# An encoder block on one core: the planner's engine durations reset, and a charge for each change of TensorE tile size

## The chip, the cores and the metric

The kernel runs on one core of a Trainium2 chip. The metric is the device time of one execution in microseconds (us). The times shown are the median and the span of several runs; the profile is of one further execution.

## What is computed

One layer of a hybrid encoder, 256 positions of 2048 features in float32. A normalised input `h` goes through one combined projection; the parts feed multi-head latent attention (8 heads), a bidirectional RWKV-7 recurrence (16 heads of 64) and gates. Both branches are projected, gated, added, projected once more, normalised and added to the input.

```python
h = rms_norm(x, g_pre)
proj = h @ w_in                       # 2048 x 10688
...
y_mla = mla_attention(q_nope, q_rope, k_nope, k_rope, v_mla)
...
def step(st, inp):                    # RWKV-7, forward and backward over time
    r_t, w_t, k_t, v_t, a_t, b_t = inp
    sa = jnp.einsum('dbhij,dbhj->dbhi', st, a_t)
    st = st * w_t[..., None, :] + sa[..., None] * b_t[..., None, :] + v_t[..., None] * k_t[..., None, :]
    y = jnp.einsum('dbhij,dbhj->dbhi', st, r_t)
    return st, y
...
u_mla = (y_mla * jax.nn.silu(z_mla)) @ w_br_mla
u_rwkv = (y_rwkv * jax.nn.silu(z_rwkv)) @ w_br_rwkv
merged = jax.nn.sigmoid(gate_mla) * u_mla + jax.nn.sigmoid(gate_rwkv) * u_rwkv
out = merged @ w_out
x = (x + rms_norm(out, g_post)).astype(x.dtype)
```

## The kernel before, in words

**Dense work.** Every projection is done with each operand split into a high and a low part, in three matmuls: high by high (L390), high by low of the input (L391), low of the weights by high (L392). Weights arrive on SP's queue in chunks of 128x1024 (three `raw` buffers). ScalarE casts a chunk to its high part `whi` (L321), VectorE subtracts to get the low part `wlo` (L324), and TensorE uses a chunk in 24 matmuls of 128x256 (`cm_task`, L390 to L392). In the text these matmuls of the shared projections are the dense matmuls. The projections after the attention norms have lines of their own: L1073 to L1082 for `wkv`, L1125 to L1127 for `wq`; the output projection has L1328 to L1330.

**The recurrence.** The 16 heads are worked in four quads, one after the other, each for both directions. For a quad, `front_k`, `front_d` and `front_v` prepare decays and keys on ScalarE and VectorE, with small matmuls for the low-rank projections (L678 to L680), head sums (L581, L582) and transposes (L642). Then `chunks_of` does, over four chunks of 64 positions:

- the Gram stage on TensorE: four times a group at L791 (64x128 tiles), masked on VectorE (L185, `g<-m,mask`), and four transposes at L799, copied by ScalarE (L778);
- the inverse of triangular 32x32 blocks on VectorE: transposes at L812 and L813, 60 small operations at L185 (`tmp`, `u`), transposes at L840, L842 and L844; then two groups of 32x32 matmuls on TensorE, L854 and L856, each copied at L861;
- the scan over the four chunks, a chain in which TensorE and the copies take turns: L886 (128x64 tiles), L906 and L908 (64x64), copies L910 and L912, L917 (64x64), copies L919 and L921, L935 and L938 (128x64), and the new state `z` (L185).

A quad's L938 must be done before the Gram stage of the next. The first `wkv` projection also waits for the last quad.

**What sets the order.** Every piece of work is a generator that yields (engine, duration, time when ready, kind) before it issues. The class `Streams` plans with these numbers: at each step it takes, for each engine, the waiting piece of best rank among those that could start within a small slot of the first, then the one that starts earliest over all engines, lets it issue, and moves that engine's free time on by the duration. A fourth field on ScalarE names the activation table, with 1.3 charged for a change. The planner runs when the program is built; each engine then works its instructions in the order in which they were issued, and waits only for data and buffers. So the durations in the source change nothing but the order. Those that the change touches are:

```python
steps.append((len(mt) * 3 * 0.109, mm) + ...)   # L394, dense step
e = yield ("P", 1.2)                            # L788, Gram group
yield ("D", cD(n * w) + 0.02)                   # L828, L830, inverse, 60 times a quad
yield ("D", 1.14)                               # L839, L841, L843, transposes
e = yield ("P", 0.9)                            # L848, 32x32 groups
e = yield ("P", 0.7, max(e0, e1))               # L913, in the scan
```

Of the kernel before, what the change touches and what calls it, by code (L numbers as in the profile page):

```python
# [16 lines left out]
D = 2048  # L17
# [26 lines left out]
class Streams:  # L44
# [32 lines left out]
    def run(self, until=None):  # L77
        while self.live and not (until and until()):
            moved = True
            while moved:  # L80
                moved = False
                for s in list(self.live):
                    while s in self.live and s[3][0] in "WT" and (s[3][0] == "T" or s[3][1]()):
                        if s[3][0] == "T":
                            s[2] = max(s[2], s[3][1])
                        self._next(s, s[2])
                        moved = True
            if until and until():
# [24 lines left out]
            self.used[e] += cost  # L113
            s[2] = start + cost + self.LAG[e]
            self._next(s, s[2])
# [33 lines left out]
def encoder_block_kernel(  # L149
# [215 lines left out]
    def cm_task(src, nk, xhi, xlo, mt, wd, end, kc=4, load_fn=None, ready=None, kready=None, k_first=0,  # L365
# [7 lines left out]
        for i, k0 in enumerate(k0s):  # L373
# [201 lines left out]
    def head_sums(v, m):  # L575
# [3 lines left out]
        yield ("P", 0.44)  # L579
# [46 lines left out]
    def front_v(Q):  # L626
# [9 lines left out]
        for q in range(0, 4, 2):  # L636
            m = yield from MB.take()
            mv = m.rearrange("p (a c) -> p a c", a=4)
            e = yield ("P", 0.45)
# [13 lines left out]
    def front_d(Q, d):  # L653
# [18 lines left out]
        for i, (t, src, bcol) in enumerate(((th, tw, V_W0F + 8 * d), (tha, ta, V_A0F + 8 * d))):  # L672
            m = yield from MB.take()
            yield ("P", 0.66)
# [86 lines left out]
    def chunks_of(Q):  # L761
# [20 lines left out]
        for d in range(2):  # L782
            for j in range(2):
# [4 lines left out]
                e = yield ("P", 1.2)  # L788
# [8 lines left out]
                e = yield ("P", 0.6)  # L797
# [13 lines left out]
        yield ("D", 2.3)  # L811
# [13 lines left out]
        for j in range(1, 31):  # L825
            n, w = 31 - j, (j + 1) // 2
            o = tmp[:, 0:n * w].rearrange("p (a b) -> p a b", b=w)
            yield ("D", cD(n * w) + 0.02)  # L828
            tt(o, bc(Ai[:, j + 1:32, j:j + 1], [128, n, w]), bc(Tc[:, j:j + 1, 0:w], [128, n, w]), ALU.mult)
            yield ("D", cD(n * w) + 0.02)  # L830
# [8 lines left out]
        yield ("D", 1.14)  # L839
        dve.transpose(out=tm[B1].rearrange("p u s -> p s u"), in_=Ai[B1].rearrange("p t s -> p s t"))  # L840
        yield ("D", 1.14)  # L841
        dve.transpose(out=Gu[B1, :, 0:32].rearrange("p u t -> p t u"), in_=Ai[B1])  # L842
        yield ("D", 1.14)  # L843
        dve.transpose(out=Gu[B2, :, 32:64].rearrange("p u t -> p t u"), in_=Ai[B2])  # L844
        for step in range(2):
# [3 lines left out]
            e = yield ("P", 0.9)  # L849
# [7 lines left out]
            for j in range(4):  # L857
                on, cost = (("A", cA(256)), ("D", cD(256)))[j % 2]
# [30 lines left out]
        for q in range(4):  # L889
# [3 lines left out]
            if q == 0:  # L893
                mu = yield from MB.take()
                pu = mu[:, 0:256].rearrange("p (a c) -> p a c", a=4)
                e = yield ("P", 0.7)
                by_v(pu, q)
            m = yield from MB.take()
            py = m[:, 0:256].rearrange("p (a c) -> p a c", a=4)
            if q:  # L900
                e = yield ("P", 0.75)
# [7 lines left out]
            e0 = yield ("A", cA(256), e)  # L909
            act.copy(rhs[Hs, 1], pu[R64[0]])  # L910
            e1 = yield ("D", cD(256), e)
            dve.tensor_copy(rhs[Hs, 0], pu[Hs])  # L912
            e = yield ("P", 0.7, max(e0, e1))  # L913
# [4 lines left out]
            e1 = yield ("A", cA(256), e)  # L918
            act.copy(uv[Hs, 0:4], pu[R64[0]])  # L919
            e2 = yield ("D", cD(256), e)  # L920
# [8 lines left out]
            e = yield ("P", 0.2 + cost + (0.5 if q < 3 else 0.0), eu)  # L929
# [107 lines left out]
    def wkv_task(g):  # L1037
# [23 lines left out]
        for k0 in range(0, 4, 2):  # L1061
# [4 lines left out]
            for k in range(k0, k0 + 2):  # L1066
# [17 lines left out]
                steps.append((12 * 0.109, mm))  # L1084
# [12 lines left out]
    def wq_task(g):  # L1097
# [8 lines left out]
        for k0 in range(0, 4, 2):  # L1106
# [11 lines left out]
            for k in range(k0, k0 + 2):  # L1118
# [10 lines left out]
                steps.append((9 * 0.109, mm))  # L1129
# [32 lines left out]
    def head(g, i):  # L1162
# [7 lines left out]
        for t in range(2):  # L1170
# [3 lines left out]
            yield ("P", 0.55)  # L1174
# [130 lines left out]
    def out_task(n, wo_v=w_out.rearrange("(k p) c -> p k c", p=128)):  # L1305
# [13 lines left out]
        for k0 in range(0, KT, 2):  # L1319
# [4 lines left out]
            for k in range(k0, k0 + 2):  # L1324
# [7 lines left out]
                for t in range(2):  # L1332
                    steps[t if n == 3 and k0 >= 6 else 0].append((3 * 0.216, lambda b, hi, lo, mm=mm, t=t: mm(b, hi, lo, t)))
# [314 lines left out]
```

## Time and profile before

| | us |
|---|---|
| median of 3 runs | 885.38 |
| lowest, highest | 884.04, 886.46 |
| the profiled execution | 883.63 |
| its span, first to last instruction | 881.9 |
| TensorE (PE) busy in the span | 851.0 |
| VectorE (DVE) busy | 660.1 |
| ScalarE (ACT) busy | 501.0 |
| mean granted TensorE clock | 0.984 of full speed |

Busy time counts a matmul from its start to its modelled end; matmuls overlap, so the step from one start to the next is what a matmul takes of the time. A row of waits has the waiting engine and line, what it waited for, the sum, the number and the longest. A row of windows has a stretch and for each engine its busy time in it, with the number of instructions; then the granted clock, the share of the DMA engines, and what they moved.

### The profile page before, as it was taken

The numbers are of one execution on the slowest core, as the hardware profiler recorded it, in microseconds if no ns is written. First come the engines' busy times: TensorE is split into PE (matmuls) and PEld (weight loads), VectorE is DVE, ScalarE is ACT, GpSimd is POOL, SyncE is SP. The second block draws the span as 40 slices with busy tenths as digits, with TensorE's granted clock in tenths as the row PEclk, the third lists the DMA queues.
The fourth block names the chain that finished last, engine by engine and source line by source line (L and its number), as shares of the span: only waits on it lengthen the run. The fifth ranks groups of instructions, "written<-read, shape, count | busy, mean of one in ns | idle before, by whom it ended". The sixth has DMA issues, their size and how long they took to land.

```text
span 881.9 us, 19393 instructions
## 1 busy us (share of the span) xinstructions
PE 851.0 (97%) x8112; PEld 814.6 (92%) x8112; DVE 660.1 (75%) x1082; ACT 501.0 (57%) x797; POOL 30.8 (3%) x66
## 2 busy tenths in 40 slices
PE   8999999999999999999999997979999999999996
PEld 8999999899999999999899896879999999998884
DVE  5878898867988867998868988566868556775554
ACT  6688554478444478554478543656857433444442
POOL 4110000000000000000001000000000000000000
PEclk9999999999999999999999999879999999999999
DMA  9566546534746534646525365125545675655563
GB/s 283 167 176 182 165 123 193 164 84 113 194 136 192 165 84 121 192 134 189 161 63 147 97 192 167 32 69 171 168 115 144 206 277 186 191 178 198 195 196 117
DMA packets 123528, 139.41 MB, mean 158 GB/s; under 512 B 6704, under 2 KB 110512, under 8 KB 123056
## 3 DMA queue, kind: packets, MB, share of 16 engines
q1 hardware_dynamic: 121664, 135.16, 51.9%
q0 software_dynamic: 768, 1.57, 0.6%
q8 instruction: 63, 1.03, 0.5%
q10 hardware_dynamic: 1008, 1.44, 0.5%
q14 instruction: 25, 0.20, 0.1%
HBM read 136.05 MB, written 2.10 MB: 157 GB/s over the span
## 4 chain that ended last, share of the span: by engine, by line
PE 88%; DVE 6%; ACT 3%; DMA 1%; issue 1%; POOL 0%; SPq 0%; DVEq 0%; ACTq 0%
PE d L390 19%; PE d L391 18%; PE d L392 18%; PE m L1329 2%; PE m L1330 2%; PE m L1328 2%; PE m L392 2%; PE m L391 2%; PE m L390 2%; PE m L791 2%; DVE wlo L324 2%; PE d L1329 1%; PE d L1330 1%; PE d L1328 1%; PE m L917 1%
## 5 line engine op out<-in xcount | busy, mean ns | idle before, releaser
L321 ACT CAST whi<-raw 128x1024 fp32r<-128x1024 f32 (+3 forms) x252 | 253.1, 1006 | 255.9 <-PE d L391 147.0
L324 DVE TENSOR_TENSOR wlo<-raw,whi 128x1024 fp32r<-128x1024 f32 (+3 forms) x250 | 292.3, 1170 | 121.2 <-ACT whi L321 119.3
L390 PE MATMUL d<-hhi,whi 128*128 128x256 f32 (+1 forms) x1264 | 366.4, 290 | 3.1 <-ACT u L1265 1.9
L392 PE MATMUL d<-hhi,wlo 128*128 128x256 f32 (+1 forms) x1264 | 358.5, 284 | 0.0
L391 PE MATMUL d<-hlo,whi 128*128 128x256 f32 (+1 forms) x1264 | 358.3, 283 | 0.1
L390 PEld LDWEIGHTS d<-hhi,whi 128*128 128x128 f32 (+1 forms) x1264 | 241.5, 191 | 7.6 <-ACT u L1265 2.1
L391 PEld LDWEIGHTS d<-hlo,whi 128*128 128x128 f32 (+1 forms) x1264 | 241.9, 191 | 0.4 <-DVE hlo L188 0.3
L392 PEld LDWEIGHTS d<-hhi,wlo 128*128 128x128 f32 (+1 forms) x1264 | 241.8, 191 | 0.3 <-DVE wlo L324 0.2
L185 DVE TENSOR_TENSOR work<-work,work 128x512 f32<-128x512 f32 (+5 forms) x64 | 38.9, 613 | 6.7 <-ACT work L429 4.5
L185 DVE TENSOR_TENSOR u<-u,tmp 128x30 f32<-128x30 f32 (+7 forms) x120 | 29.9, 250 | 3.1
L185 DVE TENSOR_TENSOR tmp<-u 128x30 f32<-128x30 f32 (+7 forms) x120 | 29.9, 249 | 3.0
L390 PE MATMUL d<-b,whi 128*128 128x256 f32 x96 | 27.1, 282 | 0.0
L392 PE MATMUL d<-b,wlo 128*128 128x256 f32 x96 | 27.1, 282 | 0.0
L392 PE MATMUL d<-ar,wlo 128*128 128x256 f32 x96 | 26.9, 281 | 0.0
L391 PE MATMUL d<-ar,whi 128*128 128x256 f32 x96 | 26.9, 280 | 0.0
L391 PE MATMUL d<-work,whi 128*128 128x256 f32 x96 | 26.9, 280 | 0.0
L390 PE MATMUL d<-ar,whi 128*128 128x256 f32 x96 | 26.9, 280 | 0.0
L1328 PE MATMUL m<-whi,hhi 128*128 128x512 f32 x60 | 23.3, 389 | 0.0
L1329 PE MATMUL m<-wlo,hhi 128*128 128x512 f32 x60 | 23.3, 389 | 0.0
L1330 PE MATMUL m<-whi,hlo 128*128 128x512 f32 x60 | 23.3, 389 | 0.0
L390 PE MATMUL m<-hhi,whi 128*128 128x256 f32 x80 | 23.2, 290 | 0.0
L392 PE MATMUL m<-hhi,wlo 128*128 128x256 f32 x80 | 22.6, 282 | 0.0
(335 smaller groups left out, 1536.9 us busy)
## 6 DMA issues: line engine op xcount, KB each, us to landing
raw<-in_w_in_dram SPq DMA_DIRECT2D x160, 512.0 KB, 3.9
raw<-in_w_out_dram SPq DMA_DIRECT2D x32, 512.0 KB, 3.6
raw<-in_w_br_mla_dram SPq DMA_DIRECT2D x16, 512.0 KB, 3.6
raw<-in_w_br_rwkv_dram SPq DMA_DIRECT2D x16, 512.0 KB, 3.4
raw<-in_mla_wkv_b_dram SPq DMA_DIRECT2D x8, 512.0 KB, 3.6
raw<-in_mla_wq_b_dram SPq DMA_DIRECT2D x8, 384.0 KB, 3.3
raw<-in_w_in_dram SPq DMA_DIRECT2D x7, 384.0 KB, 5.4
g<-in_x_dram SPq DMA_DIRECT2D x2, 1024.0 KB, 7.4
```

The costliest lines, as they stand in the source:

```text
L185: dve.tensor_tensor(out=o, in0=a, in1=b, op=op)
L321: act.copy(dst(c.hi), src(raw))
L324: eng.tensor_tensor(out=dst(c.lo), in0=src(raw), in1=dst(c.hi).bitcast(F32), op=ALU.subtract)
L390: pe.matmul(o, hi[:, c:c + m], xhi(k), start=k == k_first and i % 2 == 0, stop=False)
L391: pe.matmul(o, hi[:, c:c + m], xlo(k), start=False, stop=False)
L392: pe.matmul(o, lo[:, c:c + m], xhi(k), start=False, stop=last)
L791: pe.matmul(m[:, q * 128:q * 128 + 128], z.kb[R64[h], d, j, q], z.ar[d][R64[h], j, q], start=q == 0, stop=q == 3)
L917: pe.matmul(pu[R64[i], a], G[Hs, st, q, 0:64], rhs[Hs, st % 2, st // 2], start=a == 0, stop=a == 3)
L1328: pe.matmul(banks[t], hhi[:, k, T], hi, start=k == 0, stop=False)
L1329: pe.matmul(banks[t], hhi[:, k, T], lo, start=False, stop=False)
L1330: pe.matmul(banks[t], hlo[:, k, T], hi, start=False, stop=k == KT - 1)
```

## The change

The durations of about thirty yields are replaced. Dense matmuls go from 0.109 to 0.119 each, those of the output projection from 0.216 to 0.227. The VectorE transposes of the inverse go from 1.14 to 2.0 and its 60 small operations rise by 0.095 each; copies out of PSUM rise by 0.07 to 0.11; the small TensorE groups of the Gram stage, the inverse and the scan mostly fall. These groups now also name their tile size, and the planner charges 0.2 whenever TensorE goes from one tile size to another. No instruction's operands change. Lines after the class are 6 further down in the new kernel (L854 becomes L860).

```diff
@@ -53,6 +53,7 @@
         self.live = []
         self.used = dict.fromkeys("PADGS", 0.0)
         self.table = None
+        self.mode = "128x128"
...
@@ -106,7 +107,12 @@
             _, s, start = best
             e, cost = s[3][0], s[3][1]
-            if len(s[3]) > 3 and s[3][3] != self.table:
+            if e == "P":
+
+                mode = s[3][3] if len(s[3]) > 3 else "128x128"
+                cost += 0.2 * (mode != self.mode)
+                self.mode = mode
+            elif len(s[3]) > 3 and s[3][3] != self.table:
                 self.table = s[3][3]
                 cost += 1.3
             self.free[e] = start + cost
...
-                steps.append((len(mt) * 3 * 0.109, mm) + (((lambda k=k: kready(k)),) if kready else ()))
+                steps.append((len(mt) * 3 * 0.119, mm) + (((lambda k=k: kready(k)),) if kready else ()))
...
-                e = yield ("P", 1.2)
+                e = yield ("P", 0.9, None, "64x128")
...
-            yield ("D", cD(n * w) + 0.02)
+            yield ("D", cD(n * w) + 0.115)
...
-        yield ("D", 1.14)
+        yield ("D", 2.0)
...
-            e = yield ("P", 0.9)
+            e = yield ("P", 0.5, None, "32x32")
...
-            e = yield ("P", 0.7, max(e0, e1))
+            e = yield ("P", 0.48, max(e0, e1), "64x64")
...
```

**First place: TensorE at the inverse of quad 3.** `u` and `g` are the blocks of the inverse, `whi` and `wlo` the split weights, `hhi` and `hlo` the split input. Before:

```order
L390 MATMUL d_111<-hhi_75,whi_19_81 128x256
L391 MATMUL d_111<-hlo_76,whi_19_81 128x256
L392 MATMUL d_111<-hhi_75,wlo_22_84 128x256
L854 MATMUL m_108<-u_200_5915,g_198_5851 32x32 x32
L856 MATMUL m_109<-g_198_5851,u_200_5915 32x32 x32
L390 MATMUL d_112<-hhi_75,whi_20_82 128x256
```

Now:

```order
L398 MATMUL d_110<-hhi_75,wlo_22_84 128x256
L860 MATMUL m_107<-u_204_5657,g_198_5523 32x32 x32
L396 MATMUL d_110<-hhi_75,whi_20_82 128x256
L397 MATMUL d_110<-hlo_76,whi_20_82 128x256
L398 MATMUL d_110<-hhi_75,wlo_23_85 128x256
```

Before, the two groups of the inverse follow each other; now 24 dense matmuls stand between them, of which the first three are shown.

**Second place: TensorE at the end of the scan of quad 3.** `uv` and `work` hold the copies, `bdr` the matrix of the head sums. Before:

```order
L908 MATMUL m_107<-ar_5618,z_6780 64x64 x2
L917 MATMUL m_105<-work_131_3775,g_198_5851 64x64 x8
L938 MATMUL m_107<-g_198_5851,uv_5706 64x64 x8
L581 MATMUL m_109<-work_214_6869,bdr_68 128x256
L582 MATMUL m_109<-work_215_6870,bdr_68 128x256
```

Now:

```order
L398 MATMUL d_111<-hhi_75,wlo_22_84 128x256
L944 MATMUL m_109<-g_198_5523,uv_5483 64x64 x8
L396 MATMUL d_111<-hhi_75,whi_19_81 128x256
L397 MATMUL d_111<-hlo_76,whi_19_81 128x256
L398 MATMUL d_111<-hhi_75,wlo_22_84 128x256
```

Before, the last three steps of the chain and the head sum follow each other, and the first `wkv` matmul comes after four head-sum matmuls. Now 6 dense matmuls stand before L944 and 24 behind it, and 108 in all up to the first `wkv` matmul.

## Rows read from the trace of the kernel before

**Rows 1.** The page, busy us of each engine, its share of the span, its instructions.

```profile
PE 851.0 (97%) x8112; PEld 814.6 (92%) x8112; DVE 660.1 (75%) x1082; ACT 501.0 (57%) x797; POOL 30.8 (3%) x66
```

**Rows 2.** The page, tenths busy in 40 slices of the span, and granted clock.

```profile
DVE  5878898867988867998868988566868556775554
...
PEclk9999999999999999999999999879999999999999
```

**Rows 3.** Waits of TensorE, 480 to 600 us: total us, times, longest.

```profile
PE m L856 <- DVE g L844: 4.4, 1, 4.4
...
PE m L581 <- ACT work L429: 1.9, 1, 1.9
PE m L917 <- DVE work L912: 1.8, 1, 1.8
PE m L854 <- DVE u L840: 1.6, 1, 1.6
...
PE m L938 <- ACT uv L919: 0.8, 1, 0.8
PE m L791 <- DVE g L185: 0.7, 1, 0.7
```

**Rows 4.** Windows at quad 3: length, busy by engine (x), PEclk, DMA.

```profile
486.60:495.60 9.00, 7.10 (x83) 5.73 (x81) 9.00 (x16) 4.54 (x8) 0.00 (x0) 1.00 0.45 123
540.00:545.00 5.00, 3.36 (x86) 3.05 (x85) 4.60 (x6) 2.41 (x3) 0.00 (x0) 1.00 0.71 209
545.00:550.00 5.00, 0.49 (x5) 0.35 (x4) 4.67 (x4) 0.59 (x2) 0.00 (x0) 0.69 0.33 107
550.00:555.00 5.00, 2.84 (x68) 2.47 (x67) 1.27 (x3) 2.44 (x6) 0.00 (x0) 0.50 0.01 3
555.00:560.00 5.00, 5.00 (x55) 4.51 (x54) 0.43 (x1) 2.32 (x5) 0.00 (x0) 0.79 0.00 0
575.00:580.00 5.00, 3.27 (x88) 2.81 (x86) 3.72 (x8) 3.67 (x7) 0.61 (x2) 1.00 0.31 105
580.00:585.00 5.00, 2.23 (x33) 1.80 (x33) 4.05 (x6) 3.48 (x8) 0.00 (x0) 0.60 0.10 23
585.00:590.00 5.00, 4.86 (x23) 4.66 (x23) 3.11 (x6) 1.53 (x4) 0.00 (x0) 0.50 0.24 85
```

**Rows 5.** Windows by stage: busy PE, PEld, DVE, ACT, POOL; the sum of ten.

```profile
117.30:169.00 51.70, 51.70 (x490) 51.53 (x489) 47.35 (x92) 24.41 (x29) 0.12 (x1) 1.00 0.61 172
169.00:201.00 32.00, 30.58 (x540) 27.79 (x540) 22.00 (x38) 22.18 (x43) 2.58 (x5) 1.00 0.39 107
201.00:247.50 46.50, 46.50 (x420) 45.31 (x415) 40.27 (x57) 29.42 (x48) 1.78 (x5) 1.00 0.55 153
247.50:301.40 53.90, 53.90 (x506) 53.56 (x505) 46.16 (x86) 26.67 (x30) 0.00 (x0) 1.00 0.57 159
...
467.50:496.60 29.10, 27.20 (x251) 25.77 (x250) 25.67 (x36) 22.55 (x38) 1.10 (x3) 1.00 0.46 128
496.60:549.30 52.70, 46.77 (x446) 46.25 (x444) 47.64 (x92) 21.94 (x23) 0.00 (x0) 0.98 0.57 160
sum 431.90, PE 419.88 PEld 406.49 DVE 362.24 ACT 247.53 POOL 11.94; mean PE 41.99 PEld 40.65 DVE 36.22 ACT 24.75 POOL 1.19
```

**Rows 6.** Timeline of TensorE in quad 0's scan: start us, us, what.

```profile
176.54 0.68 PE L917 MATMUL m<-work,g 64*64 64x64 f32 x16 [0.38 <-DVE work L912]
177.15 0.38 PE L390 MATMUL d<-hhi,whi 128*128 128x256 f32 x1
...
178.33 0.28 PE L390 MATMUL d<-hhi,whi 128*128 128x256 f32 x1
178.45 0.28 PE L391 MATMUL d<-hlo,whi 128*128 128x256 f32 x1
...
178.78 0.69 PE L935 MATMUL m<-uv,b 128*64 128x64 f32 x16
```

**Rows 7.** The page, costliest groups: busy us, mean ns, idle before.

```profile
L324 DVE TENSOR_TENSOR wlo<-raw,whi 128x1024 fp32r<-128x1024 f32 (+3 forms) x250 | 292.3, 1170 | 121.2 <-ACT whi L321 119.3
```

More of the change, by code (lines that the diff above doesn't have):

```diff
@@ L578, in head_sums @@
         yield from two_parts(v, w2d(hi), w2d(lo))
-        yield ("P", 0.44)
+        yield ("P", 0.476)
         for j in range(2):
@@ L638, in front_v @@
             mv = m.rearrange("p (a c) -> p a c", a=4)
-            e = yield ("P", 0.45)
+            e = yield ("P", 0.75)
             for d, vs in ((0, v), (1, vr)):
@@ L673, in front_d @@
             m = yield from MB.take()
-            yield ("P", 0.66)
+            yield ("P", 0.715)
             for j in range(2):
@@ L796, in chunks_of @@
                 m = yield from MB.take()
-                e = yield ("P", 0.6)
+                e = yield ("P", 0.72)
                 for q in range(4):
@@ L810, in chunks_of @@
         Af = Ai.rearrange("p t s -> p (t s)")
-        yield ("D", 2.3)
+        yield ("D", 4.1)
         dve.transpose(out=Af[B1], in_=Gu[B1, :, 0:32].rearrange("p u t -> p t u"))
@@ L827, in chunks_of @@
             o = tmp[:, 0:n * w].rearrange("p (a b) -> p a b", b=w)
-            yield ("D", cD(n * w) + 0.02)
+            yield ("D", cD(n * w) + 0.115)
             tt(o, bc(Ai[:, j + 1:32, j:j + 1], [128, n, w]), bc(Tc[:, j:j + 1, 0:w], [128, n, w]), ALU.mult)
-            yield ("D", cD(n * w) + 0.02)
+            yield ("D", cD(n * w) + 0.115)
             tt(Tc[:, j + 1:32, 0:w], Tc[:, j + 1:32, 0:w], o, ALU.add)
@@ L838, in chunks_of @@
         dve.memset(Af[Hs, ::33], 1.0)
-        yield ("D", 1.14)
+        yield ("D", 2.0)
         dve.transpose(out=tm[B1].rearrange("p u s -> p s u"), in_=Ai[B1].rearrange("p t s -> p s t"))
-        yield ("D", 1.14)
+        yield ("D", 2.0)
         dve.transpose(out=Gu[B1, :, 0:32].rearrange("p u t -> p t u"), in_=Ai[B1])
-        yield ("D", 1.14)
+        yield ("D", 2.0)
         dve.transpose(out=Gu[B2, :, 32:64].rearrange("p u t -> p t u"), in_=Ai[B2])
@@ L857, in chunks_of @@
             for j in range(4):
-                on, cost = (("A", cA(256)), ("D", cD(256)))[j % 2]
+                on, cost = (("A", cA(256) + 0.07), ("D", cD(256) + 0.09))[j % 2]
                 yield (on, cost, e)
@@ L895, in chunks_of @@
                 pu = mu[:, 0:256].rearrange("p (a c) -> p a c", a=4)
-                e = yield ("P", 0.7)
+                e = yield ("P", 0.48, None, "128x64")
                 by_v(pu, q)
@@ L900, in chunks_of @@
             if q:
-                e = yield ("P", 0.75)
+                e = yield ("P", 0.5, None, "64x64")
                 for dj in range(4):
@@ L908, in chunks_of @@
                         pe.matmul(py[R64[h], dj], Z[R64[h], dj], ar[R64[h], 64:128], start=dj == 0, stop=False)
-            e0 = yield ("A", cA(256), e)
+            e0 = yield ("A", cA(256) + 0.08, e)
             act.copy(rhs[Hs, 1], pu[R64[0]])
-            e1 = yield ("D", cD(256), e)
+            e1 = yield ("D", cD(256) + 0.11, e)
             dve.tensor_copy(rhs[Hs, 0], pu[Hs])
-            e = yield ("P", 0.7, max(e0, e1))
+            e = yield ("P", 0.48, max(e0, e1), "64x64")
             for a in range(4):
@@ L917, in chunks_of @@
                     pe.matmul(pu[R64[i], a], G[Hs, st, q, 0:64], rhs[Hs, st % 2, st // 2], start=a == 0, stop=a == 3)
-            e1 = yield ("A", cA(256), e)
+            e1 = yield ("A", cA(256) + 0.08, e)
             act.copy(uv[Hs, 0:4], pu[R64[0]])
-            e2 = yield ("D", cD(256), e)
+            e2 = yield ("D", cD(256) + 0.11, e)
             dve.tensor_copy(uv[Hs, 4:8], pu[Hs])
@@ L928, in chunks_of @@
             cost = 1.0 if q < 3 else 0.5
-            e = yield ("P", 0.2 + cost + (0.5 if q < 3 else 0.0), eu)
+            e = yield ("P", cost + (0.5 if q < 3 else 0.0), eu, "128x64")
             if q < 3:
@@ L1082, in mm @@
                         pe.matmul(o, kvhl[:, 1, k, T], vh, start=False, stop=(k == 3 and t == 1))
-                steps.append((12 * 0.109, mm))
+                steps.append((12 * 0.119, mm))
             parts.append((load, plain(1024), steps))
@@ L1127, in mm @@
                         pe.matmul(o, wl, qhl[:, 0, k], start=False, stop=(k == 3 and i != 0))
-                steps.append((9 * 0.109, mm))
+                steps.append((9 * 0.118, mm))
             parts.append((load, pairs, steps))
@@ L1173, in head @@
             sc = p2(m)[:, 0]
-            yield ("P", 0.55)
+            yield ("P", 0.59)
             pe.matmul(sc, qh[:, T], kT[:, 0], start=True, stop=False)
@@ L1332, in out_task @@
                 for t in range(2):
-                    steps[t if n == 3 and k0 >= 6 else 0].append((3 * 0.216, lambda b, hi, lo, mm=mm, t=t: mm(b, hi, lo, t)))
+                    steps[t if n == 3 and k0 >= 6 else 0].append((3 * 0.227, lambda b, hi, lo, mm=mm, t=t: mm(b, hi, lo, t)))
             pairs = [(512, lambda t, i=i: half(t, i), lambda t, i=i: half(t, i)) for i in range(2)]
```

## The prediction

> **What bounds the kernel now.** I began with the page's busy table [rows 1]: TensorE is busy for 851.0 of 881.9 us, VectorE for 660.1. In the table of slices [rows 2] the eye goes to the one place where TensorE's granted clock falls below nine tenths, the 26th and 27th slice, 551 to 595 us. So the whole is a row of matmuls without gaps, except at one place. The waits of TensorE in 480 to 600 us [rows 3] name what it waits for there: VectorE's transposes L844 and L840 of the triangular inverse, and, at the end of the scan, its copies (L912, L919) and the cast for the head sum (L429). That stretch is the chain of quad 3, the last of four. The stretches of 5 us [rows 4] price it. TensorE's idle time in them is 1.90 + 1.64 + 4.51 + 2.16 + 0 + 1.73 + 2.77 + 0.14 = 14.85 us. The granted clock falls to 0.50 twice, that is to 1.2 GHz, each time after idle time; busy time multiplied by the missing share of the clock is 0.15 + 1.42 + 1.05 + 0.89 + 2.43 = 5.9 us. Not all of it is matmul time that scales, so I take 5. **About 20 us are lost at quad 3**, and next to nothing elsewhere: the same scan in quad 0 (169 to 201 us) has 32.00 - 30.58 = 1.42 us of idle time [rows 5].
>
> Why only there? The rows of a stage [rows 5] show the length of a quad: inverse 51.7 us (117.3 to 169), scan 32, then 46.5 us of finishing one quad and preparing the next. The dense projection steps fill TensorE meanwhile. In quad 3 the fill runs out: before's order has 96 dense matmuls from the first inverse matmul of quad 3 (L854) to the first wkv matmul (L1073), none of them between L854 and L856, nor after the last L938.
>
> **The price of a dense matmul.** In quad 0's scan [rows 6] L390 starts at 178.33 and L391 at 178.45: 0.12 us each. The planner had 0.109, the change says 0.119; so the new number is what the trace shows, and the planner had put 9% too little dense work beside each VectorE job. VectorE's split L324 takes 1.17 us [rows 7], one to 24 dense matmuls.
>
> **The change, part by part.** No instruction's work changes; only the order does. SP's queue, with all weight loads, stands exactly as it was. I counted the dense 128x256 matmuls of the shared projections in the two orders of TensorE.
>
> Done before L854 of quads 0 to 3: 1176, 2040, 2904, 3552 in the kernel before; 1206, 1944, 2700, 3408 (there L860) in the changed one. Quad 3's inverse thus comes 144 matmuls or 17.3 us earlier, and those 144 stand behind it: 240 instead of 96 up to wkv. 24 go between the two inverse matmul groups (before none), 24 after the second (12), 108 between the last L938 and wkv (none). 24 x 0.12 = 2.9 us beside L844 and the copies, 108 x 0.12 = 13.0 us beside the group norm and the split of kv, which TensorE now waits for.
>
> From the last Gram transposes to L854 stand 498, 504, 534 and 486 instead of 426, 438, 426 and 384. At 0.12 us that is 59.8, 60.5, 64.1 and 58.3 us for an inverse that took 51.7, 53.9 and 52.7 us on VectorE [rows 5], with 3 or 4 more splits in it (3.5 to 4.7 us). So the waits on L840 and L844 go, 1.6 + 4.4 us [rows 3]. In the Gram stage of quad 3, at 486.6 us, the 6 dense matmuls between groups that the other quads have come back, and its 1.9 us of idle time goes.
>
> *Gain.* 20 less the ordinary 1.4 of such a scan: **18.5 us**.
>
> *Loss 1, changes of tile size.* Between the 64x64 group and the 128x64 group [rows 6], 12 dense matmuls take 178.78 - 177.15 = 1.63 us instead of 1.44: 0.19 for a round trip out of one tile size and back. The new order has 140 such changes, the old 135; 2.5 round trips more are **0.5 us**. The Trainium skill, TensorEngine Tiling (Array Packing), section Tiling Modes, has a rule against more of them: "Changing tiling mode (not just tile) drains the TensorE". Charged as the planner now does, 0.2 for each change, it would make 1.0 us instead of 0.5; the trace shows about half of that, and the sum goes by the row.
>
> *Loss 2, tighter scans.* Inside a scan, from the first L886 to the last L938, the order keeps 84, 84, 72 and 84 dense matmuls where 108, 108, 108 and 84 stood; 12 more of the small projections and head sums come in for them in the first three quads. That is 12, 12, 24 and 0 fewer in all: 1.4 + 1.4 + 2.9 us less cover. If no link of the chain can be shortened, all 5.7 is waited for; if its slack takes it, none. In quad 3 the cover is only dealt out differently, with 6 instead of 12 at some copies: 0 to 2 us. Ends 0 and 7.7; I take **3**, since rows 5 show these scans with only 1.4 us of idle time, so they run near their latency.
>
> *Loss 3, VectorE.* From quad 0's inverse to the end of quad 3's, 431.9 us, VectorE is busy for 362.24 by the sum in [rows 5], 84%. The stretch now holds 2700 instead of 2802 dense matmuls (last Gram transposes of quad 0 to L854 of quad 3), 12.2 us less, and loses 12.0 us of idle time (431.9 - 419.88): some 407.7 us. VectorE sheds 102/24 splits there, 5 us: 357, or 88%. Its stages in the trace run at 47.35/51.70 = 92% in the inverse, 40.27/46.50 = 87% in the preparation, 22.00/32.00 = 69% in the scan. The new order moves front work (L692, L185) into the scan, where VectorE waits, and shrinks dense work in the preparation: from the last L938 to the next first Gram group 90, 72 and 78 dense matmuls where 258, 270 and 132 stood. In the trace VectorE held 25.67 us of work in the 29.10 before quad 3's inverse [rows 5] and TensorE then waited 0.7 us for L185 [rows 3]: a taste of what all quads may get. Lower end 0, upper end the whole gain (first rival below); I take 2 us, nearest to that 0.7 at each of three quads.
>
> ScalarE keeps its 21 table loads and its 57% load, and POOL its 30.8 us of work [rows 1]; their instructions move with the front work and the splits. I cost that at nothing: what hides it is the dense work on TensorE, and if an L321 cast came late behind front work, the next 24 dense matmuls, 2.9 us, would be late with it, which loss 3 has within its ends.
>
> *Sum.* 18.5 - 0.5 - 3 - 2 = 13 us. The profiled execution took 883.63 us: 870.6. The median of the runs shown is 885.38, so **872.4 us** by the median.
>
> **The rivals.**
>
> *VectorE does not get denser.* If it keeps its 84% in the stretch, 357/0.839 = 425.5 us stand against 407.7 that TensorE needs; 17.8 of the 18.5 us come back as waits at L854 and the Gram groups of quads 1 to 3. With the other losses: 885.4 - 18.5 + 17.8 + 3.5 = 888, **slower**. It decides at some 85% (357/(407.7 + 13) = 84.9%). For it: the scan's 69% has much waiting for other engines. Against it: that waiting is where the new order puts work, and inverse and preparation already ran at 87 to 92%. 7%.
>
> *Half of that*: 86.5% gives 412.7, 5 us of waits instead of 2, and the scan costs its full 7.7: 885.4 - 18.5 + 0.5 + 7.7 + 5 = 880. 15%.
>
> *The cover does not help*, because the first wkv step is late for another reason (the norm of kv, the copy of kr), so that the 108 matmuls only stand where the waiting was, and the wait moves behind them. Then the inverse's waits and the Gram stage's go (1.9 + 1.64 + 4.51 + 2.16 = 10.2, and half the slow clock, 2.5), the tail's 4.6 and 2.5 stay: 12.7 - 5.5 = 7, 878 us. Against it: 13 us behind the last L938 are more than before's wait there. 5%.
>
> *It does nothing that shows*: the orders differ but the same work ends last, 885. The counts speak against it. 5%.
>
> *No new waits at all*: 885.4 - 18.5 = 867, or less by what the start saves. It belongs to the forecast's own range.
>
> **How the numbers follow.** The forecast, with all between 864 and 878, has 68%, the half case 15, the slower one 7, the late wkv 5, no change 5. A measurement of this kernel tells 0.3%, 2.7 us, from no change. Faster takes the forecast, half and late-wkv cases: 0.87 with a little off for their tails; no change 0.07; slower 0.06. The range reaches from 863, where all covers hold and the start of the kernel gains a little too, to 881, which takes in the half case.
>
> **What would show it.** Right: in the profile after, the slices at 530 to 600 us show TensorE at 9 and its clock at 9; no wait of L860 or L862 (before L854, L856) for a transpose over 1 us; wkv follows dense work without a gap; the idle time of TensorE falls from 31 us to under 20; the tile-size changes show no new group of waits. Wrong: waits of TensorE for VectorE's L185 in the Gram groups, or for wlo, in quads 1 to 3, and clock below 0.9 in slices where it was full; then VectorE has become the bound. If quad 3's stall is the same size and only later, the chain was not early enough. If both the waits are gone and the time is still 885, I have misread where it went.

## The result, and the profile after

The changed kernel takes **873.12 us** (median; 872.72 to 873.52) where the kernel before takes 885.33 beside it (884.04 to 886.46). The ratio is 0.9863, with a 95% interval of 0.9845 to 0.988: 1.4% faster. The forecast was 872.4. The profiled execution took 872.72 us, its span is 870.9, its mean granted clock 0.998 (before 0.984).

First the page: busy time of each engine, then the tenths in 40 slices of the span.

```profile
PE 848.3 (97%) x8112; PEld 810.0 (93%) x8112; DVE 659.3 (76%) x1082; ACT 501.1 (58%) x797; POOL 30.7 (4%) x66
...
PE   9999999999999999999999999999999999999996
...
DVE  5878898868987878988789878775867556775554
...
PEclk9999999999999999999999999999999999999999
```

The dip of the clock [rows 2] is gone, and with it the slices in which TensorE had gaps. Every engine has as many instructions as before [rows 1]; TensorE's idle time falls from 30.9 us to 870.9 - 848.3 = 22.6. The waits of TensorE from 460 to 600 us, which answer to [rows 3]:

```profile
PE d L398 <- DVE wlo L330: 1.1, 1, 1.1
PE m L923 <- DVE work L918: 1.0, 3, 0.3
```

The transposes and the head sum are no longer in the list; of the waits for copies, 1.0 us in three pieces is left, at L923 (L917 before). The windows of quad 3 (inverse stage, scan, tail up to the first `wkv` matmul; columns as in [rows 4]):

```profile
460.50:531.80 71.30, 70.25 (x611) 69.02 (x612) 62.82 (x112) 33.55 (x41) 0.00 (x0) 1.00 0.56 157
531.80:563.60 31.80, 30.83 (x602) 27.95 (x602) 24.41 (x47) 19.48 (x39) 0.61 (x2) 1.00 0.40 113
563.60:577.50 13.90, 13.90 (x117) 13.90 (x118) 8.19 (x10) 12.02 (x17) 0.00 (x0) 1.00 0.46 150
```

The stages that had 14.85 us of idle time [rows 4] now have 1.05 + 0.97 + 0, at a clock of 1.00. The longest sums of waits in the whole execution, the start apart, are small:

```profile
PE m L923 <- DVE work L918: 3.1, 8, 0.7
PE d L398 <- DVE wlo L330: 2.3, 2, 1.2
PE m L587 <- ACT work L435: 1.3, 2, 0.7
PE m L588 <- DVE work L191: 1.2, 5, 0.3
```

**Where the time went, stage by stage.** The start of the first matmul of each stage, from the timelines, gives its length. To compare lengths that hold different numbers of matmuls, I take the change in length and subtract 0.12 us for each 128x256 matmul that came in or went out (dense, and the small ones of projections and head sums). In quads 0 to 2, 12 small projections each (L684 to L686) moved from the preparation into the scan, so the scans lost 12, 12 and 24 matmuls net, and the preparations 180, 210 and 66.

| stage | us before, after | dense before, after | change net of work, us |
|---|---|---|---|
| start to Gram stage of quad 0 | 104.7, 101.6 | 714, 672 | +1.9 |
| Gram stage to first inverse matmul, quads 0 to 2 | 62.8, 64.4, 62.7; then 71.5, 74.1, 77.3 | 462, 474, 462; then 534, 540, 576 | +2.7 |
| first inverse matmul to scan, quads 0 to 2 | 6.3, 6.2, 7.9; then 4.8, 5.2, 6.5 | 24, 24, 24; then 24, 24, 36 | -5.4 |
| scan, quads 0 to 2 | 27.2 each; then 27.0, 26.6, 26.9 | 108 each; then 84, 84, 72 | +4.6 |
| last L938 to next Gram stage | 34.6, 36.0, 19.4; then 14.7, 12.7, 11.8 | 258, 270, 132; then 90, 72, 78 | +3.9 |
| quad 3, its tail, and on to the output projection | 299.5, 314.8 | 1632, 1914 | -18.6 |

The sum is -10.9, the spans differ by 11.0. The last row is the forecast gain. The rows above it hold the losses: that of the start, for which the prediction had no term, and those of VectorE (second and fifth row) and of the tighter scans. The third row is a gain that the prediction had not.

### The profile page after: what moved, and what is told of

It is laid out like the page before. It is cut to its first block, busy times and chain, and to the rows that moved or that the text cites. A ratio compares the mean times of both kernels' runs of the same rounds, so it can differ in the third digit from the quotient of the medians.

```text
span 870.9 us, 19398 instructions
## 1 busy us (share of the span) xinstructions
PE 848.3 (97%) x8112; PEld 810.0 (93%) x8112; DVE 659.3 (76%) x1082; ACT 501.1 (58%) x797; POOL 30.7 (4%) x66
## 4 chain that ended last, share of the span: by engine, by line
PE 73%; DVE 14%; ACT 8%; issue 2%; DMA 2%; DVEq 0%; ACTq 0%
PE d L396 16%; PE d L398 16%; PE d L397 15%; DVE wlo L330 4%; PE m L1334 2%; PE m L1335 2%; PE m L1336 2%; ACT whi L327 2%; DVE work L191 2%; PE m L398 2%; PE m L396 2%; PE m L397 2%; PE d L1335 1%; PE d L1334 1%; PE d L1336 1%
## 5 line engine op out<-in xcount | busy, mean ns | idle before, releaser
L396 PE MATMUL d<-hhi,whi 128*128 128x256 f32 (+1 forms) x1296 | 375.1, 289 | 0.0
L398 PE MATMUL d<-hhi,wlo 128*128 128x256 f32 (+1 forms) x1296 | 366.5, 283 | 2.3 <-DVE wlo L330 2.3
L397 PE MATMUL d<-hlo,whi 128*128 128x256 f32 (+1 forms) x1296 | 366.2, 283 | 0.0
L396 PEld LDWEIGHTS d<-hhi,whi 128*128 128x128 f32 (+1 forms) x1296 | 246.8, 190 | 4.5
L398 PEld LDWEIGHTS d<-hhi,wlo 128*128 128x128 f32 (+1 forms) x1296 | 246.9, 190 | 2.7 <-DVE wlo L330 2.7
L397 PEld LDWEIGHTS d<-hlo,whi 128*128 128x128 f32 (+1 forms) x1296 | 247.1, 191 | 0.1
L191 DVE TENSOR_TENSOR work<-work,work 128x512 f32<-128x512 f32 (+5 forms) x64 | 38.8, 612 | 3.9 <-ACT work L575 1.2
L191 DVE TENSOR_TENSOR u<-u,tmp 128x30 f32<-128x30 f32 (+7 forms) x120 | 29.9, 250 | 3.0
L191 DVE TENSOR_TENSOR tmp<-u 128x30 f32<-128x30 f32 (+7 forms) x120 | 29.8, 249 | 2.9
L397 PE MATMUL d<-work,whi 128*128 128x256 f32 x96 | 26.9, 280 | 0.0
L397 PE MATMUL d<-ar,whi 128*128 128x256 f32 x96 | 26.9, 280 | 0.0
L191 DVE TENSOR_TENSOR g<-m,mask 128x512 f32<-128x512 f32 x32 | 20.6, 686 | 0.0
L797 PE MATMUL m<-ar,u 64*128 64x128 f32 x256 | 19.2, 285 | 0.3 <-DVE g L191 0.3
```

Of the source, the lines that this page charges most:

```text
L191: dve.tensor_tensor(out=o, in0=a, in1=b, op=op)
L797: pe.matmul(m[:, q * 128:q * 128 + 128], z.kb[R64[h], d, j, q], z.ar[d][R64[h], j, q], start=q == 0, stop=q == 3)
```

## The experiments

Twelve kernels, in three batches, each beside the kernel before (884.83, 884.4 and 884.65 us).

**How much cover the tail needs.** `GPRE` is the number of gate groups, 96 dense matmuls each, that are issued before the attention instead of inside it. In the changed kernel, one fewer leaves 12 dense matmuls behind the last L944, one more 204.

```diff
-GPRE, MIX = 4, [0, 1, 1, 1]
+GPRE, MIX = 3, [0, 1, 1, 1]
```

> The changed kernel (873.1 us), but one gate task of 96 dense matmuls is moved from before the wkv projection to behind it: 12 dense matmuls instead of 108 stand between the last L944 of quad 3 and the first wkv matmul; all else up to there is the same order. Theory 'cover': the wait of the kernel before at this place comes back in part. There, about 3.5 us of idle time (4.6 us from L938 to wkv less 1.1 of work) and some 2.5 us of slow clock were lost; 12 matmuls cover 1.4. So 2 to 4.5 us slower, 875 to 877.6, with a wait of TensorE at the head sum and a clock below 1 in the slice of 565 to 585 us. Rival 'the tail is worth nothing, since the wait only moves behind the dense work': 872.5 to 873.7, no change.

881.08 us, ratio 0.9967 (0.9952 to 0.9982). The first row is from the waits of TensorE, the others are windows behind the last L944:

```profile
PE m L587 <- ACT work L435: 4.6, 4, 3.0
...
563.60:568.60 5.00, 3.38 (x34) 2.64 (x32) 2.89 (x5) 3.94 (x8) 0.00 (x0) 1.00 0.30 108
568.60:573.60 5.00, 1.99 (x8) 1.79 (x9) 3.27 (x5) 2.87 (x6) 0.00 (x0) 0.75 0.20 52
573.60:578.60 5.00, 5.00 (x28) 5.00 (x27) 0.69 (x1) 3.14 (x5) 0.00 (x0) 0.57 0.14 52
```

The wait for the head sum's cast is back, and after two windows with 1.62 and 3.01 us of idle time the granted clock is 0.57, near the lower level, while TensorE is fully busy. The stretch up to `wkv` takes 8.7 us with 12 dense matmuls where it took 14.1 with 108, 8.7 - (14.1 - 96 x 0.12) = 6.1 us more than its work; the next, to the output projection, 211.5 - (197.8 + 96 x 0.12) = 2.2 us more. So the cover is worth 8.3 us, more than I expected of it: idle time of 4.6 us and the slow clock behind it.

The same with five groups:

```diff
-GPRE, MIX = 4, [0, 1, 1, 1]
+GPRE, MIX = 5, [0, 1, 1, 1]
```

> The changed kernel with one gate task more ahead of wkv: 204 instead of 108 dense matmuls behind the last L944, and 96 fewer in the attention stage. Theory 'cover is a shared stock, and 108 is enough': nothing is gained at wkv, and the attention stage waits for its softmax as in the run before with this move: 873.5 to 877. Rival '108 is still short': 869 to 872.

879.5 us, 0.9949 (0.9929 to 0.9969), above the expected range. The tail has no wait with 108, and none with 204. But the attention lost 96 matmuls of its own cover: it takes 190.9 us for 1056 dense matmuls instead of 197.8 for 1152, 4.6 us more than 0.12 each explains, and a wait appears that the changed kernel does not have:

```profile
PE m L1203 <- DVE work L197: 2.4, 2, 2.2
```

And the kernel before with five groups, of whose 96 extra matmuls the planner put 42 into quad 3's scan and 54 behind it:

```diff
-GPRE, MIX = 4, [0, 1, 1, 1]
+GPRE, MIX = 5, [0, 1, 1, 1]
```

> The kernel before (885.3 us), but one gate task of 96 dense matmuls is moved ahead of wkv: the order up to L854 of quad 3 is that of before (3552 dense matmuls, none between L854 and L856), then 138 instead of 96 stand in the scan of quad 3 and 54 instead of none behind it. Theory 'cover': the tail's part of the loss goes (2.8 + 1.7 us of idle time, 2.5 of slow clock, 4 to 7 us together), the inverse's part stays (1.9 + 1.6 + 4.5 + 2.2 us): 878 to 881. Rival 'the gain comes from better interleaving in quads 0 to 2': 884.5 to 886, no change.

882.83 us, 0.9984 (0.9964 to 1.0004): no change that can be told, and less than the theory expected.

```profile
PE m L856 <- DVE g L844: 4.4, 1, 4.4
...
PE m L1197 <- DVE work L191: 2.4, 2, 2.1
...
PE m L854 <- DVE u L840: 1.6, 1, 1.6
```

The tail's wait is gone here too, but the inverse's waits stay and the attention waits instead. **Dense work is one stock.** In these two runs, cover that was taken from the attention was paid for there; what the change does is to deal it out better.

This run has one more use. Up to the inverse of quad 3 its order of TensorE is that of the kernel before, so the two profiles show one order in two executions. From the first inverse matmul to the scan, first in the kernel before (quads 0 and 1), then here (quads 0 to 2):

```profile
167.50:173.80 6.30, 5.26 (x153) 4.62 (x152) 5.32 (x7) 2.63 (x6) 0.00 (x0) 1.00 0.41 119
300.10:306.30 6.20, 5.32 (x153) 4.62 (x152) 5.21 (x7) 2.66 (x6) 0.00 (x0) 1.00 0.62 170
...
167.70:174.80 7.10, 6.05 (x153) 5.26 (x152) 5.90 (x8) 3.42 (x7) 0.00 (x0) 0.88 0.43 117
301.40:308.50 7.10, 6.22 (x153) 5.48 (x152) 5.90 (x8) 3.49 (x8) 0.00 (x0) 0.84 0.62 166
434.50:442.60 8.10, 6.63 (x155) 5.84 (x154) 6.67 (x9) 3.54 (x8) 0.00 (x0) 0.80 0.60 160
```

The idle time is the same, 1.05 and 0.88 us in quads 0 and 1, but here the granted clock falls behind it and there it does not.

**The parts of the change.** The changed kernel without the charge:

```diff
-                cost += 0.2 * (mode != self.mode)
+                cost += 0.0 * (mode != self.mode)
```

> The changed kernel with the charge for a change of tile size set from 0.2 to 0; all measured durations stay. 137 changes of tile size instead of 140. The planner then reaches quad 3's inverse after 3552 dense matmuls, as the kernel before did, with none between the two inverse groups and none behind the last L944. Theory 'cover': nearly the whole loss of the kernel before at quad 3 is back (12 to 20 us): 884 to 890. Rival 'measured durations make the gain, the charge is a detail': 872 to 875.

889.49 us, 1.0046 (1.0029 to 1.0062), as the theory had it: 3552 of the 3648 dense matmuls up to `wkv` are used up before L860 of quad 3, as in the kernel before, and the waits there are back and, in sum, longer.

```profile
PE m L860 <- DVE u L846: 5.2, 1, 5.2
PE d L396 <- ACT work L549: 4.9, 1, 4.9
PE m L862 <- DVE g L850: 2.7, 1, 2.7
```

The kernel before with the charge alone (0.2 and the tile sizes, old durations; lines 5 further down):

```diff
+            if e == "P":
+                mode = s[3][3] if len(s[3]) > 3 else "128x128"
+                cost += 0.2 * (mode != self.mode)
+                self.mode = mode
...
```

> The kernel before with the charge of 0.2 alone, all its old durations. Quad 3's inverse comes after 3312 dense matmuls (240 earlier than before, 96 earlier than in the changed kernel), 216 stand behind the last L938. From the last Gram transposes to L854 stand 426, 414, 474 and 414 dense matmuls: 51.1, 49.7, 56.9, 49.7 us for an inverse of 51.7 to 53.9. Theory 'cover': quad 3's loss goes as in the changed kernel; the inverse waits 1 to 4 us in three quads: 873 to 881. Rival 'the inverse's measured durations are needed, VectorE is the bound': waits of over 5 us at L854 in each quad, 885 or more.

878.99 us, 0.9943 (0.9922 to 0.9964): about half of the gain.

The kernel before with the new dense durations alone:

```diff
-                steps.append((len(mt) * 3 * 0.109, mm) + ...
+                steps.append((len(mt) * 3 * 0.119, mm) + ...
...
```

> The kernel before (885.3 us) with the new durations of dense matmuls alone (0.119 and so on), no charge, old inverse durations. Quad 3's inverse comes after 3102 dense matmuls (450 earlier), 420 stand behind its last L938; from the last Gram transposes to L854 stand 390, 402, 408 and 366, 46.8 to 49.0 us. By the same theory: the loss at quad 3's end is gone (10 us), but 3 to 6 us of waits come at L854 or L856 in each quad: 880 to 890. Rival 'the dense duration is what the change is worth': 872 to 875.

879.39 us, 0.9954 (0.9929 to 0.9978), just under the range expected. It leaves 420 matmuls behind the last L938, so quad 3 is covered; but L856 waits for the copies L861 in all quads, 6.2 us in 8 waits, and from the first inverse matmul to the end of the scan quads 0 and 1 take 38.7 and 40.1 us, with 144 dense matmuls in them, where the kernel before takes 33.6 and 33.4 with 132.

The changed kernel with the old durations in the inverse (all its transposes, the first two too, and the 60 small operations):

```diff
-        yield ("D", 4.1)
+        yield ("D", 2.3)
...
-            yield ("D", cD(n * w) + 0.115)
+            yield ("D", cD(n * w) + 0.02)
...
-        yield ("D", 2.0)
+        yield ("D", 1.14)
```

> The changed kernel (873.1 us) with the old durations of the VectorE inverse (transposes 1.14, small operations 0.095 less), all else as changed, the charge too. From the last Gram transposes to L860 stand 390, 408, 408 and 372 dense matmuls instead of 498, 504, 534 and 486: 46.8, 49.0, 49.0 and 44.6 us for an inverse that takes 50 to 54 with 16 splits in it; 528 instead of 108 stand between the last L944 and wkv. Theory 'the inverse needs dense work beside it of its own length': TensorE waits 3 to 6 us at L860 or L862 in each of the four quads, partly with a slow clock, while the end of quad 3 stays covered: 881 to 890. Rival 'only the cover behind quad 3 counts': 872 to 874.

887.11 us, 1.0024 (1.0003 to 1.0044), in the expected range, but for a reason I had not named: there is cover of 528 matmuls behind quad 3, and yet L862 waits 6.1 us in 8 waits for the copies L867, in every quad. TensorE's idle time from L860 to the scan is 1.6 to 2.7 us a quad and not the 3 to 6 expected; but in quads 1 to 3 the granted clock there is 0.70 to 0.73, and the four stretches take 41.0 us instead of 24.0 with as many dense matmuls (132). That led to the next one: the transposes alone.

```diff
-        yield ("D", 2.0)
+        yield ("D", 1.14)
```

> The changed kernel with the three transposes of the inverse (L846, L848, L850) planned at 1.14 us again instead of 2.0, all else as changed. The planner then believes VectorE done 2.6 us earlier and puts L860 nearer to, or before, the end of L850, so that the first copies L867 queue on VectorE behind it and behind a split. Cover at quad 3 stays: 72 dense matmuls behind the last L944. Theory (part of the gain is the place of L860 against L850): waits of L862 for the copies L867 come back, some 1 to 1.5 us a quad, and the time is 877 to 881 us. Rival (the 60 small operations' durations and the dense one set the order, the transposes do not matter): L862 waits under 0.5 us a quad, 872 to 875 us.

884.75 us, 1.0008 (0.9997 to 1.0019): the whole gain is gone, more than the theory said, and the rival falls. To see how, take the inverse of quad 0 in three timelines. Before (VectorE, ScalarE, TensorE):

```profile
166.97 1.99 DVE L844 STREAM_TRANSPOSE g<-u 32x1024 f32<-32x1024 f32 x1
168.99 1.23 DVE L324 TENSOR_TENSOR wlo<-raw,whi 128x1024 fp32r<-128x1024 f32 x1
170.25 0.42 DVE L861 COPY u<-m 32x256 f32<-32x256 f32 x1
171.10 0.43 DVE L861 COPY u<-m 32x256 f32<-32x256 f32 x1 [0.43 <-ACT u L861]
...
170.70 0.36 ACT L861 COPY u<-m 32x256 f32<-32x256 f32 x1 [1.77 <-DVE u L861]
...
167.50 0.75 PE L854 MATMUL m<-u,g 32*32 32x32 f32 x64
...
170.72 0.24 PE L856 MATMUL m<-g,u 32*32 32x32 f32 x2 [0.67 <-DVE u L861]
```

After (VectorE, ScalarE, TensorE):

```profile
170.91 2.04 DVE L850 STREAM_TRANSPOSE g<-u 32x1024 f32<-32x1024 f32 x1
172.97 1.23 DVE L330 TENSOR_TENSOR wlo<-raw,whi 128x1024 fp32r<-128x1024 f32 x1
174.24 0.42 DVE L867 COPY u<-m 32x256 f32<-32x256 f32 x1
...
173.84 0.36 ACT L867 COPY u<-m 32x256 f32<-32x256 f32 x1 [0.48 <-PE m L860]
...
173.05 0.75 PE L860 MATMUL m<-u,g 32*32 32x32 f32 x64
...
175.35 0.92 PE L862 MATMUL m<-g,u 32*32 32x32 f32 x64
```

With the transposes at 1.14 (VectorE, TensorE, and the window from there to the scan):

```profile
171.17 2.00 DVE L850 STREAM_TRANSPOSE g<-u 32x1024 f32<-32x1024 f32 x1
173.20 1.23 DVE L330 TENSOR_TENSOR wlo<-raw,whi 128x1024 fp32r<-128x1024 f32 x1
174.46 0.42 DVE L867 COPY u<-m 32x256 f32<-32x256 f32 x1
...
171.12 0.75 PE L860 MATMUL m<-u,g 32*32 32x32 f32 x64
...
174.93 0.24 PE L862 MATMUL m<-g,u 32*32 32x32 f32 x2 [1.27 <-DVE u L867]
...
171.10:180.90 9.80, 8.16 (x165) 7.49 (x164) 7.57 (x10) 4.54 (x9) 0.77 (x2) 0.83 0.48 126
```

On VectorE the row is the same each time: last transpose, one split, first copy. What moves is L860 (L854). A planner that takes a transpose for 1.14 us puts the group 0.5 us after the real start of the last transpose (before), or beside it; its result then lies until transpose and split are done, 2.75 us or 3.34 us from the group's start to VectorE's first copy. With 2.0 the group comes 2.14 us after the transpose began, and the copy 1.19 us after the group. When the result lies longer, TensorE runs out of the dense matmuls that stand between the two groups and waits, and the clock falls: 0.83 in this window and 0.84, 0.88 and 0.84 in the same one of the other quads, where the changed kernel has 1.00 in all. The four stretches from the first inverse matmul to the scan take 9.8, 8.7, 9.1 and 9.5 us instead of 4.8, 5.2, 6.5 and 7.5 with about as much dense work (126 matmuls, 132): 13.1 us more in all, of which 7.2 are idle time (7.6 instead of 0.4). That is more than the 11.6 us by which the run is slower than the changed kernel.

**Neighbours.** If cover at quad 3 and the place of the inverse groups were all, small shifts of the numbers should cost little.

```diff
-                cost += 0.2 * (mode != self.mode)
+                cost += 0.3 * (mode != self.mode)
```

> The changed kernel with a charge of 0.3 instead of 0.2. Quad 3's inverse comes after 3366 dense matmuls (42 earlier), 192 stand behind its last L944; inverses have 498, 510, 516 and 492 beside them; the scans keep 78, 72, 60 and 60 dense matmuls from the first L892 on instead of 84, 84, 72 and 84. Theory: quad 3 is covered as before, the tighter scans and preparations cost 1 to 4 us: 873 to 877. Rival 'the earlier the chain the better': under 872.

884.39 us, 0.9994 (0.9982 to 1.0006): a clear miss. So three more neighbours: the charge at 0.15 and 0.25, and the dense matmul at 0.121.

```diff
-                cost += 0.2 * (mode != self.mode)
+                cost += 0.15 * (mode != self.mode)
```

> The changed kernel with a charge of 0.15 instead of 0.2. In its order 102 dense matmuls stand behind the last L944, 3432 before L860 of quad 3, and the copies of the inverse have one split among them as in the changed kernel. Theory (cover at quad 3 and the place of the copies set the time): 872 to 876 us. Rival (small details of one order decide, as the charge of 0.3 with 884 suggests): 879 to 886 us.

**869.94 us**, 0.9842 (0.9826 to 0.9858), the fastest of all, and better than expected.

```diff
-                cost += 0.2 * (mode != self.mode)
+                cost += 0.25 * (mode != self.mode)
```

> The changed kernel with a charge of 0.25. 144 dense matmuls behind the last L944, 3384 before L860 of quad 3; two splits ahead of the copies in quad 0. Scans of 72 to 96 dense matmuls, between the changed kernel's and those of the charge of 0.3. Theory: cover is there, a little more waiting in the scans, 873 to 878 us. Rival (details of one order decide): 879 to 886 us.

879.15 us, 0.9943 (0.9927 to 0.9958): above the theory's range and at the lower end of the rival's.

```diff
-                steps.append((len(mt) * 3 * 0.119, mm) + ...
+                steps.append((len(mt) * 3 * 0.121, mm) + ...
```

> The changed kernel with 0.121 instead of 0.119 for each dense matmul of the shared projections. 114 dense matmuls behind the last L944, 3408 before L860 of quad 3, inverse stages of 528 to 558. Theory (cover at quad 3 and the place of the copies): 871 to 876 us. Rival (details of one order decide): 879 to 886 us.

875.05 us, 0.9901 (0.9887 to 0.9916), as the theory had it.

All four have cover behind quad 3 (192, 102, 144 and 114 matmuls) and little waiting of L862 for copies, 1.3 us at most. What tells them apart is, for the most part, the scan. First the charge of 0.15, from the waits of TensorE:

```profile
PE m L923 <- DVE work L918: 1.1, 3, 0.4
```

The charge of 0.25:

```profile
PE m L923 <- DVE work L918: 4.0, 8, 0.8
...
PE m L912 <- DVE z L191: 1.9, 4, 0.8
...
PE m L944 <- ACT uv L925: 1.2, 2, 0.8
```

The charge of 0.3, and one of its windows in quad 2:

```profile
PE m L923 <- DVE work L918: 4.7, 10, 1.0
PE d L398 <- DVE wlo L330: 3.6, 3, 2.5
PE m L912 <- DVE z L191: 2.0, 5, 0.6
...
356.00:361.00 5.00, 4.69 (x26) 4.69 (x27) 4.39 (x10) 2.07 (x4) 0.00 (x0) 0.66 0.71 207
```

At L923 the waits are 1.1, 3.1 (the changed kernel), 3.5 (0.121), 4.0 and 4.7 us, and the times 869.9, 873.1, 875.1, 879.2 and 884.4 go in the same order. That holds among these five only: the kernel before with the charge alone waits 5.4 us there (its L922) at 878.99 us, and the run with the old transposes 1.4 us at 884.75.

The lengths of the scans say more than the waits. The four scans take 27.0, 26.6, 26.9 and 24.1 us in the changed kernel; with 0.25 they take 28.9, 27.8, 28.8 and 28.8 with as many dense matmuls in the first two and 12 more in each of the last. Net of work, 0.12 us for each 128x256 matmul, that is 6.8 us more, of the 7.2 by which the spans of the two profiles differ. By the same reckoning the scans hold 3.0 of the 3.1 us that the charge of 0.15 gains, 0.8 of the 2.0 that 0.121 loses, and 7.2 of the 12.1 that 0.3 loses. Another 4.0 us of those 12.1 lie between the Gram stage and the inverse of quad 2, where one wait for `wlo` of 2.5 us is followed by a granted clock of 0.66. So it is shown where the neighbours differ; which step of the planner's choice at 0.25 and 0.3 makes the worse scans was not tried.

## Why the prediction was right, and where it was not

*The gain at quad 3*, 18.5 forecast, is **18.6** by the table. The idle time, the slow clock and the chain of quad 3 were read rightly from [rows 3] and [rows 4], and the 108 matmuls behind the last L944 do cover group norm and `kv` split. The two parts are each a little off, and the errors cancel: idle time fell by 12.8 us (14.85 to 2.02) where 13.45 was forecast, and the other 5.8 us are near the 5.9 worked out for the slow clock, of which 5 was taken. The run with 12 of them rules out the rival "cover does not help"; its loss costs 8.3 us.

*The planner's numbers are the lever*: shown. The charge alone and the dense numbers alone each give about half of the gain. Without the charge the other parts make the kernel slower than before (889.49 us), and without the new transposes the whole gain is lost (884.75). The parts do not add.

*Loss 1*, more changes of tile size, 0.5 us: it is too small to be told apart inside the stages of the table. No new group of waits came with the 140 changes, as the prediction had said.

*Loss 2*, tighter scans, taken at 3 (ends 0 and 7.7): **4.6** in quads 0 to 2. That is inside the ends. 12 to 24 matmuls fewer, 1.4 to 2.9 us of work, made the scans only 0.2 to 0.7 us shorter, so most of the cover that was taken away was waited for.

*Loss 3*, VectorE, taken at 2 (ends 0 and 17.8): **6.6** by the table, 2.7 in the inverse stages and 3.9 in the preparation. This term was mis-sized. Idle time makes up 3.8 us of it. The waits name some of its links: in quads 0 to 2 the split `wlo` (1.2 us; the other 1.1 of its 2.3 us falls in quad 3, the last row of the table) and the head sum behind the scan (L587 and L588, 1.9 us). In quad 0 the planner put 24 dense matmuls, 2.9 us, behind the last L944, while the cast for the head sum comes 3.7 us behind it (the first of the 24 starts at 204.97, L587 at 208.66 after 0.56 us of waiting for the cast). I took the 0.7 us of one Gram group as the price of a quad, though the preparation lost 54 to 198 dense matmuls of cover. What the 2.8 us that are not idle time consist of was not found.

*The step that failed outright* is the sentence that next to nothing is lost outside quad 3. Its evidence was misread: of the 1.42 us of idle time from 169 to 201 us, which I took for the ordinary idle time of a scan, 1.04 us is L856 waiting for the copies L861, before the scan begins (6.30 - 5.26 in the window from 167.50 shown above); the scan itself has 0.38. In quads 1 and 2 L856 waited for these copies too, and in quad 2 the granted clock had dipped to 0.85, too briefly for a slice of [rows 2]. Two rows of before, from its waits and its windows, and the same stretch of quad 2 after:

```profile
PE m L856 <- DVE u L861: 3.1, 7, 1.1
...
432.20:440.10 7.90, 6.40 (x154) 5.60 (x152) 6.70 (x9) 3.56 (x8) 0.00 (x0) 0.85 0.56 150
...
415.30:421.80 6.50, 6.31 (x166) 5.81 (x164) 5.88 (x9) 4.34 (x10) 0.00 (x0) 1.00 0.56 158
```

Idle time in these stretches of quads 0 to 2 falls from 3.4 to 0.4 us, and the dip of the clock is gone; that is most of the **5.4 us** that the table shows as gained, and the forecast had no term for it. It nearly cancels the part by which losses 2 and 3 were larger (1.6 and 4.6), so it is partly luck that the forecast total came close. The profile of before may even show too little of this loss: in the second execution of the same order, shown above, the three stretches take 22.4 us instead of 20.4. This fits that the medians differ by 12.2 us and the two profiles by only 11.0.

*The start* cost 1.9 us more than its work, where the prediction hoped that it might gain. This is not the spread of the first loads. Less 0.12 us a dense matmul, the three kernels with 714 matmuls ahead of the first Gram stage (the kernel before, alone, with five gate groups and with the charge) take 17.7 to 18.2 us from their first matmul to that stage; the ten with 672 take 19.9 (the changed kernel) to 23.0. So the orders with fewer matmuls there are longer net of work each time. Why was not found.

*The first rival's arithmetic*: from 113.4 to 531.6 us, the same stages, VectorE is busy for 354.78 of 418.2 us, 84.8%. So it hardly became denser, and by the rival that meant slower, 888; yet the kernel is faster. The stretch of [rows 5] was the wrong yardstick: it ends at 549.3, after the wait at L856 had begun, while the new order's ends at L860. Before, the stretch to L854 (544.25) was 427.0 us, with VectorE busy for 357.27, or 83.7%. About 5 us of the shortening that I asked of VectorE thus lay outside the stretch. Since the share rose by about one point only, the runs do not show whether VectorE could have gone higher.

*What would show it*: the slices, the missing waits on transposes (L862 waits 0.4 us in all, for a copy) and the gapless tail came as said. TensorE's idle time under 20 us did not: it is 22.6. That sign did not follow from the prediction's own sum, which gives 30.9 - 13.45 + 3 + 2 = 22.5 with its losses 2 and 3. Of the wrong signs, the waits for `wlo` came (2.3 us, in quads 1 and 3), but the clock stayed at 1.00 behind them, and the Gram groups waited 0.3 us for L191 (L185 before); VectorE did not become the bound.

## What to carry to other kernels

Where a planner orders the work, look first for the stage in which its filler runs out, and count filler there, before and after, in matmuls: one number (108 matmuls behind the last step of the chain, or none) showed where the time went when the engine's busy share did not. It is not enough alone: runs with 192 and 528 matmuls there took 884 and 887 us. Then look at every place where a short matmul group hands over to a busy engine: with a duration that is too short (1.14 for 2.0) the group ran before its reader was free, and the next group waited for the reader. Read a wait to the engine that ends it before calling it a stage's ordinary idle time. And do not trust one order: neighbours of the same numbers ran from 870 to 884 us, so a table of durations is to be tried with its neighbours, and the best one kept (here a charge of 0.15, 3 us better than the change).

## What was not expected of the hardware

A wait of TensorE cost up to twice its length. With 12 matmuls of cover, 4.6 us of idle time in two windows were followed by a window at a granted clock of 0.57, and 8.3 us were lost in all. With the old transposes, waits of L862 of 1.8 us at most went with a clock of 0.83 to 0.88 in the windows of all four inverses, and 7.2 us of idle time with 13.1 us of added length.

Whether the clock falls is not fixed by the order. The same order of TensorE up to quad 3, with the same idle time at L856, had a granted clock of 1.00 in quads 0 and 1 in one execution and of 0.88 and 0.84 in another.

The copies of one group never ran side by side. The four copies L867 of a group alternate: ScalarE's first lasts from 173.84 to 174.20, VectorE's starts at 174.24, and each of the later ones waits for the one before it on the other engine (1.77 and 0.43 us at L861 in the rows of before). So a copy that is late behind a split holds up all that follow it, on both engines. The Trainium skill, PSUM — Partial Sum Buffer, section PSUM bank collisions raise a hardware error, says that two engines on one bank and the same quadrant (32 rows) collide, reads among themselves included, and that the hardware does not make one of them wait; on different quadrants of one bank, it says, the same pairs run clean. These four copies read four different quadrants (`pm[32 * j:32 * j + 32]`), so by that section their reads need not take turns. The trace shows only that they do, by waits that the program contains; whether they could run side by side, and what the shorter hand-over would be worth, no run here shows.
